# Turning the linear attention's decayed keys and output by VectorE and DMA instead of TensorE, with another split of the transfers and longer pauses

## The chip, the cores and the metric

The kernel runs on one core of one Trainium2 chip. The metric is device time in microseconds (us) of one execution. A core has TensorE (PE; its weight loads are listed apart as PEld), VectorE (DVE), ScalarE (ACT), GpSimd (POOL) and SyncE (SP), and 16 DMA engines that move data between the on-chip memory and DRAM. [...]

## The reference

Two layers, each on 256 rows of width 2048. One input projection feeds three groups of heads: A, eight heads of chunked soft-max attention; B, four heads of gated linear attention; M, four heads of cross-attention into 256 memory rows. Each group is multiplied by a SiLU gate, and one output projection and a normalisation close the layer. What matters here is group B:

```python
def step(state, inp):
    qc, kc, vc, gc = inp
    b = jnp.cumsum(gc, axis=1)
    decay = jnp.exp(-jnp.abs(b[:, :, None] - b[:, None, :]))
    attn = jnp.einsum('bihd,bjhd,bijhd->bhij', qc, kc, decay)
    o_intra = jnp.einsum('bhij,bjhv->bihv', attn, vc)
    o_inter = jnp.einsum('bihd,bhdv->bihv', qc * jnp.exp(b), state)
    b_last = b[:, -1]
    k_dec = kc * jnp.exp(b_last[:, None] - b)
    new_state = jnp.exp(b_last)[..., None] * state + jnp.einsum('bjhd,bjhv->bhdv', k_dec, vc)
    return new_state, o_intra + o_inter
...
h = x @ w_in
...
o_b = o_b * lax.rsqrt(jnp.mean(jnp.square(o_b), axis=-1, keepdims=True) + RMS_EPS) * gla_norm_g.astype(jnp.float32)
...
y = jnp.concatenate([y_a * jax.nn.silu(a_z), y_b * jax.nn.silu(b_z), y_m * jax.nn.silu(m_z)], axis=-1)
out = y @ w_out
return layer_norm(DEEPNORM_ALPHA * x + out, ln_g, ln_b)
```

`k_dec` has features in partitions when it is made, and the product over `j` needs positions there, so it must be turned. The gated output `y_b` has positions in partitions, and the output projection wants features there, so it is turned too.

## The kernel before, in words

The large projections run in **pieces**. A piece loads a slab of weights by a DMA on SP's queue (`piece`, L129), splits it into a high part (`wh`, cast by ScalarE, L117) and a low part (`wl`, by VectorE, L118), and multiplies both with the activations on TensorE (`mm`, L95). The pools of `raw`, `wh` and `wl` have four buffers each. In a layer the pieces come in the order: memory values and keys, B's queries and keys, four groups of value columns (`values`, 388 columns each), between them A's queries and keys for two groups of four heads, the memory queries, B's gate, three more gate projections, and four groups of the output projection. A group has eight pieces.

The small work (attention heads and linear attention) is put between the pieces by generators. After each piece the code calls `tick` (L52), which adds 1 to a clock (0.76 for a value piece) and lets at most one due generator run to its next `yield`; the number it yields is how many ticks it pauses. While the linear attention runs two generators are active, after that three; a finished one makes room for the next. `finish` ticks without pieces until the given generators are done. Since TensorE and SP keep the program's order, the pauses set where the small products stand in TensorE's stream. VectorE, ScalarE and GpSimd are not in that list: their order is made by a scheduler when the program is built, from dependences, priorities and its own estimate of times. In the text below pieces are counted within a layer from the first piece of B's queries and keys.

`gla` (L312) is the linear attention: gates, the cumulative sum `b_`, the decayed keys `kd` (L367 to L371), a pause of 6, then four TensorE transposes of `kd` into a PSUM bank (L397), a ScalarE copy to `kdT` (L399), a pause of 2, and the state products from `kdT`. `gla_gate` (L482) multiplies the output by its gate, and `gla_turned` (L491) turns it by eight TensorE transposes (L498) into two banks, from which ScalarE makes the scaled high part (L501) and VectorE the low part (L502) of the output projection's first operand.

`a_head` (L516) is a chunk head: scores on TensorE, soft-max on VectorE and ScalarE, `turned`, a pause of 7, then the value products from `pT` and a pause of 2. `m_head` (L546) is a memory head: scores, soft-max, `turned`, a pause of 7, two casts of `pT` (ScalarE) and two subtractions (VectorE), a pause of 2, products.

`turned` (L505) turns a tile of four 128-row blocks without TensorE: VectorE transposes each 32x32 square in one instruction (L508), and transfers through a DRAM tile `home` put the squares in their place. They are issued by GpSimd: four writes of 32 partitions each (L511), then, when they have landed, one read of the whole (L512).

Of the kernel before, what the change touches and what calls it, by code (L numbers as in the profile page):

```python
# [8 lines left out]
F32 = mybir.dt.float32  # L9
# [3 lines left out]
AF = mybir.ActivationFunctionType  # L13
ALU = mybir.AluOpType
# [4 lines left out]
P = 128  # L19
D = 2048  # L20
T = 256
L = 2
CH = 64
# [13 lines left out]
def hybrid_trunk_kernel(  # L37
# [7 lines left out]
    pe, dve, act, pool, sp = nc.tensor, nc.vector, nc.scalar, nc.gpsimd, nc.sync  # L45
# [27 lines left out]
    def enter(name, bufs=1, **kw):  # L73
        return ctx.enter_context(tc.tile_pool(name=name, bufs=bufs, **kw))
# [5 lines left out]
    hd = enter("hd", 1)  # L80
# [9 lines left out]
    def nm(s):  # L90
        uid[0] += 1
        return f"{s}_{uid[0]}"

    def mm(o, l, r, start, stop):
        pe.matmul(o, l, r, start=start, stop=stop, skip_group_check=True)  # L95

    def bank():
        return psa.tile([P, 512], F32, name=nm("bk"), tag="bk")

    def scratch(shape, dtype=F32):  # L100
        return sc.tile(shape, dtype, name=nm("sc"), tag="sc")

    def small(shape, tag, bufs=1):
        return sm.tile(shape, F32, name=nm(tag), tag=tag, bufs=bufs)

    ident = cst.tile([P, P], F32, name="ident")
# [3 lines left out]
    def operand():  # L110

        x = opp.tile([P, 4, 2, T], F32R, name=nm("x"), tag="x")
        return x[:, :, 0], x[:, :, 1], x.rearrange("p j h t -> p j (h t)")
# [198 lines left out]
    def gla(gw, gb, ng, gq, gk, lr, asv, yraw):  # L312
        gqf = gq.rearrange("p b t -> p (b t)")
        gkf = gk.rearrange("p b t -> p (b t)")
        pairs = [hd.tile([P, 4, CH], F32, name=nm("pairs"), tag=f"pairs{par}") for par in range(2)]

        def products(kl, ql, pb):

# [23 lines left out]
        pt = bank()  # L342
# [24 lines left out]
        kd = scratch([P, 512])  # L367
# [5 lines left out]
        act.activation(eb, b_, AF.Exp, scale=1.0 / 16)  # L373
        elast = small([P, 8], "elast")
        dve.tensor_copy(elast, eb.rearrange("p (g c) -> p g c", c=CH)[:, :, CH - 1])
        qe = hd.tile([P, 512], F32, name=nm("qe"), tag="qe")
        dve.tensor_tensor(qe, gqf, eb, op=ALU.mult)
        yield 6

        def decayed(s):  # L380

# [9 lines left out]
            return kl, ql  # L391


        pt = bank()
        for t in range(2):
            for b in range(2):
                pe.transpose(pt[:, (t * 2 + b) * P:(t * 2 + b + 1) * P], kd[:, b * T + t * P:b * T + t * P + P], ident)  # L397
        kdT = scratch([P, 4, P])
        act.copy(kdT, pt.rearrange("p (g c) -> p g c", c=P))  # L399
        yield 2  # L400
        nxt = [decayed(LEVELS[0])]
        kv = [bank() for _ in range(2)]
        for c in range(3):
            rs = slice((c % 2) * 64, (c % 2) * 64 + 64)
            t = c // 2
            for b in range(2):
                for par in range(2):
                    h = 2 * b + par
                    mm(kv[c % 2][par * 64:par * 64 + 64, (t * 2 + b) * P:(t * 2 + b + 1) * P],
                       kdT[rs, t * 2 + b, par * 64:par * 64 + 64],  # L410
                       asv[rs, t, 16 + h * P:16 + (h + 1) * P], True, True)

        low, high = bank(), bank()
        diagonal, first = [low[:, :256], kv[1][:, 256:]], [low[:, 256:], high[:, :256]]
        products(gkf, gqf, diagonal)
        products(*nxt[0], first)
        st = hd.tile([P, 3, 2, P], F32, name=nm("st"), tag="st")
        for c in range(3):
            t = c // 2
            src = kv[c % 2].rearrange("p (g c) -> p g c", c=P)[:, t * 2:t * 2 + 2]  # L420
# [19 lines left out]
        on = [yraw[:, 2 * par:2 * par + 2].rearrange("p c (g d) -> p (c g) d", d=P) for par in range(2)]  # L440
# [8 lines left out]
        for t in range(2):  # L449
            for b in range(2):  # L450
                g = t * 2 + b
# [5 lines left out]
        for odd, even in ((1, 2), (3, None)):  # L457
            for b in range(2):
                for c in (odd, even):
                    if c is not None:  # L460
                        for par in range(2):
                            g = (c // 2) * 2 + b
# [4 lines left out]
        for par in range(2):  # L467
# [3 lines left out]
            r = on[par][at[half], 2 - 2 * half:]  # L471
# [18 lines left out]

    def gla_turned(yraw, ng, y):  # L491

        for par in range(2):
            on = yraw[:, 2 * par:2 * par + 2].rearrange("p t (b d) -> p t b d", d=P)
            pt = bank()
            for t in range(2):
                for b in range(2):
                    pe.transpose(pt[:, b * T + t * P:b * T + (t + 1) * P], on[:, t, b], ident)  # L498
            ptv = pt.rearrange("p (b t) -> p b t", b=2)
            hi, lo = (x.rearrange("p (b r) t -> p r b t", r=2)[:, par] for x in y[:2])  # L500
            act.activation(hi, ptv, AF.Copy, scale=ng[:, 0:1])  # L501
            dve.scalar_tensor_tensor(lo, ptv, ng[:, 0:1], hi.bitcast(F32), op0=ALU.mult, op1=ALU.subtract)  # L502
            yield 1

    def turned(dst, src, n):  # L505

        blocks = scratch([P, 4, n])
        dve.transpose(blocks.rearrange("p b (g j) -> p g b j", j=32), src.rearrange("p (g b j) -> p g b j", b=4, j=32))  # L508
        home = drm.tile([P, 4, n], F32, name=nm("home"), tag=f"home{n}")
        for a in range(4):  # L510
            pool.dma_start(home[:, a].rearrange("(b i) n -> i b n", b=4), blocks[a * 32:(a + 1) * 32])  # L511
        pool.dma_start(dst, home)  # L512

    SCALE = P ** -0.5

    def a_head(h, load_bias, bias, q, k, asv, y):  # L516

        if h + 2 < 8:
            load_bias(h + 2)
        pb = bank()  # L520
        mm(pb[:, 0:128], q[:, 0:128], k[:, 0:128], True, True)
        mm(pb[:, 128:384], q[:, 128:256], k, True, True)
        s = scratch([P, 384])
        dve.scalar_tensor_tensor(s, pb[:, :384], SCALE, bias[h], op0=ALU.mult, op1=ALU.add)  # L524
        mx = small([P, 2], "mx", 4)
        zs = small([P, 2], "zs", 4)
        own = (slice(0, 128), slice(128, 384))
        for t in range(2):
            dve.tensor_reduce(mx[:, t:t + 1], s[:, own[t]], AX.X, ALU.max, negate=True)  # L529
        for t in range(2):  # L530
            act.activation(s[:, own[t]], s[:, own[t]], AF.Exp, bias=mx[:, t:t + 1], accum_out=zs[:, t:t + 1])  # L531
        dve.reciprocal(zs, zs)
        for t in range(2):
            dve.tensor_scalar(s[:, own[t]], s[:, own[t]], zs[:, t:t + 1], None, op0=ALU.mult)
        pT = tp.tile([P, 4, 96], F32, name=nm("pT"), tag="pT")
        turned(pT, s, 96)
        yield 7
        po = bank()
        v0 = 528 + h * P
        pv, pov = pT.rearrange("p a (g j) -> p g a j", j=32), po[:, :256].rearrange("p (t a j) -> p t a j", t=2, j=32)  # L540
        mm(pov, asv[:, 0, v0:v0 + P], pv[:, 0:2], True, False)
        mm(pov[:, 1], asv[:, 1, v0:v0 + P], pv[:, 2], False, True)
        act.copy(y, po[:, :256])
        yield 2

    def m_head(h, q, mk, mv, y):  # L546
# [17 lines left out]
        for t in range(2):  # L564
            dve.tensor_scalar(s[:, t], s[:, t], zs[:, t:t + 1], None, op0=ALU.mult)
        pT = hd.tile([P, 4, 128], F32, name=nm("pT"), tag="qe" if h % 2 else "gb_")
        turned(pT, s.rearrange("p t m -> p (t m)"), 128)
        yield 7
        ph, pl = scratch([P, 2, 256], F32R), scratch([P, 2, 256], F32R)
# [50 lines left out]
    def columns(n):  # L620
        return slice(n * 512, (n + 1) * 512)

    def wo_pieces(l, n):

        if n < 3:
            return [w512[l, G_WO + n, pc] for pc in range(8)]
        return [[w256[l, i, pc // 2][:, pc % 2 * 512:pc % 2 * 512 + 512] for i in range(2)] for pc in range(8)]
# [141 lines left out]
    for l in range(L):  # L769
# [20 lines left out]
        gq = hd.tile([P, 2, T], F32, name=nm("gq"), tag="gq")  # L790
        gk = hd.tile([P, 2, T], F32, name=nm("gk"), tag="gk")
# [17 lines left out]
        def heads(g):  # L809
            t = hd.tile([P, 4, T], F32, name=nm("qk"), tag="qk", bufs=4)  # L810
            for i, a, b in ws_group(w512[l, g], xq):
                total(t[:, i:i + 2], a, b)
            return t
# [14 lines left out]
        def load_bias(h):  # L828
            bias[h] = hd.tile([P, 384], F32, name=nm("bias"), tag="bias", bufs=4)
            sp.dma_start(bias[h], relw[l, h])  # L830
# [3 lines left out]
        if l > 0:  # L834
            finish(gens)
        yraw = [per.tile([P, 4, T], F32, name=nm("yr"), tag=f"yr{i}") for i in range(4)]
        gens = [[gla(*gp, gq, gk, lr, asv, yraw[0])]]
        waiting.extend(gens[0])
        linear[:] = gens[0]
        for half in range(2):  # L840
            values(2 + half)
            q = heads(G_AQ0 if half == 0 else G_AQ1)
            k = heads(G_AK0 if half == 0 else G_AK1)
# [14 lines left out]
        gla_gate(acc, yraw[0])  # L858
        yq = [operand()]
        gens[0] = [gla_turned(yraw[0], gp[2], yq[0])]  # L860
        waiting[:0] = gens[0]
        for i, g in ((1, G_AZ0), (2, G_AZ1), (3, G_MZ)):
            y = operand()
# [18 lines left out]
        for n in range(WO_N):  # L882
            if last:
                g, b = scratch([P, 512]), scratch([P, 512])
            else:
                both = per.tile([P, 2, 512], F32, name=nm("gb"), tag=f"yr{n}")
                g, b = both[:, 0], both[:, 1]
# [3 lines left out]
            src = wo_pieces(l, n)  # L891
# [30 lines left out]
            if last:  # L922
                r = res[:, 1, columns(n)]
# [90 lines left out]
```

## Time and the profile before

| | |
|---|---|
| median of 3 runs | 922.42 us (922.07 to 927.72) |
| the profiled execution's own time | 922.5 us |
| its span in the profile | 920.7 us |
| TensorE busy | 909.6 us, 99% |
| VectorE, ScalarE, GpSimd busy | 65%, 53%, 10% |
| mean granted TensorE clock | 0.995 |
| DMA | 189 MB, 206 GB/s |

The span is what the profiler saw from the first to the last instruction; the execution's own time has 1.8 us more around it. Lines of the profile name the kernel's line, the engine, the operation and the tiles as written by the program (`sc` is any scratch tile, `bk` a PSUM bank, `acc` a projection's accumulator, `yr` the heads' outputs). In the views by line the numbers after the bar are busy us, the mean ns of one, and the idle time of the engine just before, with what ended it. In the waits they are us in total, the number of waits, and the longest. In the chain a row has its start, its length and what it was. In the stretches of time each engine has its busy us and its number of instructions, then come the granted clock, the DMA share and GB/s.

### The profile page before, as it was taken

Reading aid. Unit: us, or ns where it says so; the run is one execution under the profiler, and the core shown is the slowest. Engines: PE = TensorE matmul, PEld = TensorE weight load, DVE = VectorE, ACT = ScalarE, POOL = GpSimd, SP = SyncE. Lnnn points to the kernel's source line nnn. Section 1 sums busy time; section 2 is a strip of 40 time slices with the busy share of each in tenths; the row PEclk is TensorE's granted clock in tenths of the full one; section 3 lists DMA queues with packets and bytes.
Section 4 is the critical chain, followed back from the end, with each engine's and each line's share of the span. In section 5 each row is a group of like instructions: output and inputs, shape, how many; then the busy total and the mean of one; then the engine's idle time right before and its main releaser. Section 6 shows DMA issues by size and latency. Waiting matters only on the chain.

```text
span 920.7 us, 14332 instructions
## 1 busy us (share of the span) xinstructions
PE 909.6 (99%) x5420; PEld 798.8 (87%) x5420; DVE 602.2 (65%) x845; ACT 488.7 (53%) x702; POOL 87.8 (10%) x169
## 2 busy tenths in 40 slices
PE   9999999999999999999999999999989999999997
PEld 7889998998888888888888899889878888888885
DVE  6764478656566576555587665985746676776566
ACT  6644475475455565434476445654734565654350
POOL 1000000012033030000000000001211230310000
PEclk9999999999999999999999999999999999999998
DMA  9965865558576586655774466555565775776652
GB/s 306 335 191 173 297 219 165 157 178 278 170 216 203 200 252 205 216 195 184 233 255 164 152 205 202 186 163 179 209 212 175 220 214 177 228 251 208 199 162 91
DMA packets 75989, 189.33 MB, mean 206 GB/s; under 512 B 9224, under 2 KB 33160, under 8 KB 75664
## 3 DMA queue, kind: packets, MB, share of 16 engines
q1 hardware_dynamic: 69120, 173.30, 57.7%
q0 software_dynamic: 6656, 14.86, 5.5%
q8 instruction: 42, 0.69, 0.3%
q10 hardware_dynamic: 144, 0.26, 0.1%
q14 instruction: 27, 0.22, 0.1%
HBM read 181.01 MB, written 7.34 MB: 205 GB/s over the span
## 4 chain that ended last, share of the span: by engine, by line
PE 90%; DMA 4%; ACT 2%; DVE 1%; issue 1%; POOL 1%; SPq 0%; POOLq 0%
PE acc L95 82%; PE bk L95 7%; DMA home<-sc 2%; DMA raw<-w 2%; DMA pT<-home 1%; ACT wh L117 1%; POOL home L511 1%; ACT sc L474 1%; PE bk L599 0%; DVE wl L118 0%; ACT L290 0%; PE bk L498 0%; ACT asv L807 0%; DVE mx L529 0%; DVE qk L263 0%
## 5 line engine op out<-in xcount | busy, mean ns | idle before, releaser
L118 DVE TENSOR_TENSOR wl<-raw,wh 128x1024 fp32r<-128x1024 f32 (+3 forms) x321 | 369.9, 1154 | 251.6 <-ACT wh L117 250.3
L117 ACT CAST wh<-raw 128x1024 fp32r<-128x1024 f32 (+3 forms) x321 | 318.9, 995 | 338.1 <-PE acc L95 231.8
L95 PE MATMUL acc<-x,wh 128*128 128x512 f32 x1248 | 397.1, 400 | 0.2 <-ACT wh L117 0.2
L95 PE MATMUL acc<-wh,x 128*128 128x512 f32 (+2 forms) x1236 | 356.5, 369 | 0.0
L95 PEld LDWEIGHTS acc<-x,wl 128*128 128x128 f32 x1248 | 234.7, 188 | 55.3
L95 PEld LDWEIGHTS acc<-wh,x 128*128 128x128 f32 x1236 | 227.0, 188 | 27.8 <-ACT wh L117 0.4
L95 PE MATMUL acc<-x,wl 128*128 128x256 f32 x1248 | 246.0, 278 | 0.0
L95 PE MATMUL acc<-wl,x 128*128 128x512 f32 (+2 forms) x618 | 228.0, 369 | 0.0
L95 PEld LDWEIGHTS acc<-x,wh 128*128 128x128 f32 x1248 | 192.6, 189 | 2.5 <-ACT wh L117 0.8
L95 PEld LDWEIGHTS acc<-wl,x 128*128 128x128 f32 x618 | 116.0, 188 | 15.0 <-DVE wl L118 0.8
L511 POOL DMA_DIRECT2D home<-sc x96 | 52.5, 554 | 336.6 <-DVE sc L508 333.5
L531 ACT ACTIVATE sc<-sc,mx 128x128 f32<-128x128 f32 (+1 forms) x32 | 14.3, 448 | 10.6 <-DVE mx L529 10.5
L512 POOL DMA_DIRECT2D pT<-home x24 | 13.4, 560 | 54.2 <-DMA home<-sc 49.8
L95 PE MATMUL bk<-pT,asv 128*128 128x256 f32 (+1 forms) x64 | 14.0, 342 | 4.2 <-DMA pT<-home 4.2
L95 PEld LDWEIGHTS bk<-pT,asv 128*128 128x128 f32 x64 | 11.7, 197 | 5.9 <-DMA pT<-home 4.6
L386 ACT ACTIVATE sc<-sc 128x512 f32<-128x512 f32 x12 | 7.6, 633 | 15.4 <-DVE sc L384 15.3
L508 DVE STREAM_TRANSPOSE sc<-sc 128x384 f32<-128x384 f32 (+1 forms) x24 | 14.9, 621 | 0.6
L118 DVE TENSOR_TENSOR x<-sc,x 128x512 fp32r<-128x512 f32 x20 | 13.3, 684 | 0.7 <-ACT x L117 0.7
L304 POOL DMA_DIRECT2D gwraw<-gate_w x6 | 3.1, 522 | 106.0 <-PE bk L587 105.1
L95 PE MATMUL bk<-qk,qk 128*128 128x128 f32 (+1 forms) x64 | 13.1, 326 | 0.0
L118 DVE TENSOR_TENSOR x<-res,x 128x512 fp32r<-128x512 f32 (+2 forms) x14 | 10.4, 764 | 4.0 <-ACT x L117 4.0
L524 DVE SCALAR_TENSOR_TENSOR sc<-bk,bias 128x384 f32<-128x384 f32 x16 | 8.7, 543 | 6.6 <-PE bk L95 6.5
(207 smaller groups left out, 566.3 us busy)
## 6 DMA issues: line engine op xcount, KB each, us to landing
raw<-w SPq DMA_DIRECT2D x214, 512.0 KB, 4.3
raw<-w SPq DMA_DIRECT2D x64, 388.0 KB, 3.5
raw<-w SPq DMA_DIRECT2D x83, 256.0 KB, 3.5
bias<-relw SPq DMA_DIRECT2D x16, 192.0 KB, 4.2
home<-sc POOLq DMA_DIRECT2D x64, 48.0 KB, 3.7
pT<-home POOLq DMA_DIRECT2D x16, 192.0 KB, 4.1
res<-xT SPq DMA_DIRECT2D x4, 512.0 KB, 5.0
res<-xn SPq DMA_DIRECT2D x1, 2048.0 KB, 8.2
```

What stands on the lines that cost most here:

```text
L95: pe.matmul(o, l, r, start=start, stop=stop, skip_group_check=True)
L117: act.copy(hi, src)
L118: dve.tensor_tensor(lo, src, hi.bitcast(F32), op=ALU.subtract)
L304: pool.dma_start(raw[i * 16:i * 16 + 16], gate_w[l])
L386: act.activation(dd, dd, AF.Abs)
L474: act.activation(sq, on[par][:, g], AF.Square, scale=1.0 / math.sqrt(P), accum_out=ms[:, par * 4 + g:par * 4 + g + 1])
L508: dve.transpose(blocks.rearrange("p b (g j) -> p g b j", j=32), src.rearrange("p (g b j) -> p g b j", b=4, j=32))
L511: pool.dma_start(home[:, a].rearrange("(b i) n -> i b n", b=4), blocks[a * 32:(a + 1) * 32])
L512: pool.dma_start(dst, home)
L524: dve.scalar_tensor_tensor(s, pb[:, :384], SCALE, bias[h], op0=ALU.mult, op1=ALU.add)
L531: act.activation(s[:, own[t]], s[:, own[t]], AF.Exp, bias=mx[:, t:t + 1], accum_out=zs[:, t:t + 1])
```

## The change

The decayed keys are turned by `turned` instead of TensorE, right after they are made; the pause behind them is 9 instead of 6; ScalarE's copy to `kdT` reads the landed tile with the 32-wide squares reordered, and the state products take `kdT` with the indices of half and pair exchanged. `pairs` is allocated later. The gated output is turned by two calls of `turned`, each with a pause of 6, and the scaled high and low parts are made in four steps of 128x128 each for either half, from the landed tiles. `turned` itself now makes one write of the whole tile and four reads of 32 partitions each. A chunk head pauses 9 ticks instead of 7.

```diff
@@ gla
-        pairs = [hd.tile([P, 4, CH], F32, name=nm("pairs"), tag=f"pairs{par}") for par in range(2)]
+        pairs = []
...
+        kdm = hd.tile([P, 4, P], F32, name=nm("kdT"), tag="st")
+        turned(kdm, kd, P)
         qe = hd.tile([P, 512], F32, name=nm("qe"), tag="qe")
         dve.tensor_tensor(qe, gqf, eb, op=ALU.mult)
-        yield 6
+        yield 9
...
-        pt = bank()
-        for t in range(2):
-            for b in range(2):
-                pe.transpose(pt[:, (t * 2 + b) * P:(t * 2 + b + 1) * P], kd[:, b * T + t * P:b * T + t * P + P], ident)
         kdT = scratch([P, 4, P])
-        act.copy(kdT, pt.rearrange("p (g c) -> p g c", c=P))
+        act.copy(kdT.rearrange("p g (a j) -> p g a j", j=32), kdm.rearrange("p a (g j) -> p g a j", j=32))
...
-                       kdT[rs, t * 2 + b, par * 64:par * 64 + 64],
+                       kdT[rs, b * 2 + t, par * 64:par * 64 + 64],
...
+        pairs.extend(hd.tile([P, 4, CH], F32, name=nm("pairs"), tag=f"pairs{par}") for par in range(2))
@@ gla_turned
+        yT = []
         for par in range(2):
-            on = yraw[:, 2 * par:2 * par + 2].rearrange("p t (b d) -> p t b d", d=P)
-            pt = bank()
+            yT.append(hd.tile([P, 4, P], F32, name=nm("yT"), tag=("gq", "gk")[par]))
+            turned(yT[par], yraw[:, 2 * par:2 * par + 2].rearrange("p t d -> p (t d)"), P)
+            yield 6
+        for par in range(2):
             for t in range(2):
                 for b in range(2):
-                    pe.transpose(pt[:, b * T + t * P:b * T + (t + 1) * P], on[:, t, b], ident)
-            ptv = pt.rearrange("p (b t) -> p b t", b=2)
-            hi, lo = (x.rearrange("p (b r) t -> p r b t", r=2)[:, par] for x in y[:2])
-            act.activation(hi, ptv, AF.Copy, scale=ng[:, 0:1])
-            dve.scalar_tensor_tensor(lo, ptv, ng[:, 0:1], hi.bitcast(F32), op0=ALU.mult, op1=ALU.subtract)
+                    hi, lo = (x.rearrange("p k (t a j) -> p k t a j", t=2, j=32)[:, b * 2 + par, t] for x in y[:2])
+                    src = yT[par].rearrange("p a (t b j) -> p t b a j", t=2, j=32)[:, t, b]
+                    act.activation(hi, src, AF.Copy, scale=ng[:, 0:1])
+                    dve.scalar_tensor_tensor(lo, src, ng[:, 0:1], hi.bitcast(F32), op0=ALU.mult, op1=ALU.subtract)
             yield 1
@@ turned
-        for a in range(4):
-            pool.dma_start(home[:, a].rearrange("(b i) n -> i b n", b=4), blocks[a * 32:(a + 1) * 32])
-        pool.dma_start(dst, home)
+        pool.dma_start(home, blocks)
+        for b in range(4):
+            pool.dma_start(dst[b * 32:(b + 1) * 32], home[:, b].rearrange("(a i) n -> i a n", a=4))
@@ a_head
         turned(pT, s, 96)
-        yield 7
+        yield 9
```

## The prediction

> **What bounds the kernel now.** I read the page's busy times and clock first, then the waits, then the chain that ended last in order of time.
>
> ```profile
> span 920.7 us, 14332 instructions
> PE 909.6 (99%) x5420; PEld 798.8 (87%) x5420; DVE 602.2 (65%) x845; ACT 488.7 (53%) x702; POOL 87.8 (10%) x169
> ...
> PEclk9999999999999999999999999999999999999998
> ```
>
> TensorE is never short of work except for 11 us of the span. The waits say where:
>
> ```profile
> PEld bk L95 <- DMA pT<-home: 4.6, 2, 3.0
> ...
> PE acc L95 <- ACT wh L117: 0.2, 1, 0.2
> ACT wh L117 <- PE acc L95: 231.8, 163, 2.8
> ```
>
> There are two real waits in the middle of the program, one per layer, and both are for pT, a chunk head's turned probabilities (4.6 us by the weight loads, which are the first to be held). Everything else feeds TensorE in time: ScalarE's weight cast waits 163 times for TensorE to free a buffer, so ScalarE is as far ahead as four buffers let it be. So time can be won in two ways only: fewer TensorE instructions, or those two waits. The chain gives both their place:
>
> ```profile
> 132.49 0.44 PE bk L397 x4
> ...
> 175.87 2.12 PE acc L95 x12
> ...
> 226.60 3.44 DMA pT<-home
> 230.08 0.92 PE bk L95 x4
> 231.00 16.73 PE acc L95 x96
> ...
> 251.83 2.78 PE acc L95 x16
> 254.62 0.66 PE bk L95 x4
> ...
> 316.84 0.44 PE bk L498 x4
> ...
> 323.32 0.71 PE bk L95 x6
> ...
> 679.01 4.75 DMA pT<-home
> 683.81 1.65 PE bk L95 x4
> 685.46 17.33 PE acc L95 x96
> ```
>
> Four transposes take 0.44 us of TensorE; a piece of 16 products takes 2.78, one of 12 narrow ones 2.12; a chunk head's score or value products 0.66, a memory head's 0.71. The wait at 230.08 and that at 683.81 stand before the same thing, the value products of chunk head 3: counted by the tick rule they come after six pieces (x96) and before the scores of head 4. The second wait costs more than itself. The same four products then take 1.65 instead of 0.92 us and the next 96 take 17.33 instead of 16.73: 1.3 us. The clock shows why:
>
> ```profile
> 683.80:687.20 3.40, 3.39 (x12) 2.93 (x13) 0.00 (x0) 0.37 (x1) 0.00 (x0) 0.58 0.52 169
> 230.10:233.50 3.40, 3.40 (x19) 2.99 (x20) 0.69 (x1) 0.37 (x1) 0.00 (x0) 1.00 0.63 223
> ```
>
> After the 3.0 us wait the granted clock was 0.58 over 3.4 us and 12 matmuls went through; after the shorter wait of layer 0 it stayed 1.00. [...]
>
> **The change, part by part.** *Transposes removed.* Each layer loses four at L397 and eight at L498, 24 in all, six groups of 0.44 us: **-2.6 us**. All lie between products of the pieces, on the path. No matmul is added: the products that read kdT are the same with another index.
>
> *What takes their place.* Per layer three turnings more (kd, and the output twice): three VectorE transposes of 128x512, 15 GpSimd DMAs, and ScalarE and VectorE work on other operands.
>
> ```profile
> L508 DVE STREAM_TRANSPOSE sc<-sc 128x512 f32<-128x512 f32 x8 | 5.7, 710 | 0.2
> L501 ACT ACTIVATE x<-bk,ng 128x512 fp32r<-128x512 f32 x4 | 2.7, 684 | 0.0
> L502 DVE SCALAR_TENSOR_TENSOR x<-bk,ng,x 128x512 fp32r<-128x512 f32 x4 | 3.0, 744 | 0.0
> L474 ACT ACTIVATE sc<-yr x16: 303/311/313, 192.8 to 649.7; 128x128 f32<-128x128 f32 x16
> ```
>
> VectorE gains 3 x 0.71 us per layer. The kdT copy stays one instruction. The two 128x512 steps on each engine in the output become eight of 128x128; no row has that form, and between a quarter of 684 ns (no cost per instruction) and the 311 ns of a 128x128 square on ScalarE (L474) lie the bounds; I take 0.35, a little over the upper one for the stepped source: 2.8 instead of 1.4 us on each engine per layer. Cover: ScalarE is busy 53%, VectorE 65%, and both only have to stay ahead of TensorE by the weight buffers. **0**, as long as neither is held.
>
> kd's chain: the turning starts some 0.7 us after kd, and its first consumer now comes nine pieces later instead of six, plus two as before. Write, wait, reads and landing add up to 0.55 + 4 + 2.2 + 4, about 11 us, from the rows below, and nine pieces of 2.12 us are 19 us at the least. GpSimd has nothing else then:
>
> ```profile
> 181.90 2.20 POOL L511 DMA_DIRECT2D home<-sc  x4 [63.52 <-DVE sc L508]
> ```
>
> It sits idle for 63.5 us before the first head's turning at 181.9. **0**.
>
> The pauses move everything behind them on TensorE: I counted the ticks again. gla ends four pieces later (at the 61st piece of the layer's tick count instead of the 57th), chunk heads 1, 2, 3 then issue their scores in pieces 61, 62, 63 (before 57, 59, 60) and their value products in 70, 71, 72 (before 64, 66, 67). Heads 4 to 7 and the memory heads follow two pieces later than before, and the last step of the output falls in the last piece but one of the gates (111 of 112). Nothing spills into an emptied `finish`, so TensorE has a piece to work on at each step.
>
> *A turning with one write and four reads.* Same five issues, same bytes.
>
> ```profile
> home<-sc POOLq DMA_DIRECT2D x64, 48.0 KB, 3.7
> pT<-home POOLq DMA_DIRECT2D x16, 192.0 KB, 4.1
> ```
>
> An issue takes GpSimd about 0.55 us (the timeline rows further down, four in 2.2); the large transfer lands in 4.1 us and the small in 3.7; which is the write changes the sum by nothing I can see: 0.55 + 4.1 + 2.2 + 3.7 against 2.2 + 3.7 + 0.55 + 4.1. TensorE must now wait on four landings per head instead of one; a semaphore instruction there takes 51 ns:
>
> ```profile
> L599 PEldq EVENT_SEMAPHORE  x4: 51/51/51, 476.4 to 489.6; - x4
> ```
>
> Three more for 16 chunk heads is 2.4 us at most if each is felt, 0 if they run while the array is busy, as this row's four do: they appear nowhere among TensorE's waits. I take 0.
>
> *The wait of chunk head 3.* This is the largest term, so here is the chain on GpSimd (timeline of POOL, layer 0):
>
> ```profile
> 203.43 2.21 POOL L511 DMA_DIRECT2D home<-sc  x4 [12.61 <-DVE sc L508]
> 208.59 0.56 POOL L512 DMA_DIRECT2D pT<-home  x1 [2.94 <-DMA home<-sc]
> 212.66 2.18 POOL L511 DMA_DIRECT2D home<-sc  x4 [3.50 <-DVE sc L508]
> 218.92 0.56 POOL L512 DMA_DIRECT2D pT<-home  x1 [4.08 <-DMA home<-sc]
> 219.47 2.18 POOL L511 DMA_DIRECT2D home<-sc  x4
> 226.60 0.56 POOL L512 DMA_DIRECT2D pT<-home  x1 [4.95 <-DMA home<-sc]
> ```
>
> the score products of heads 1, 2 and 3 on TensorE:
>
> ```profile
> 196.72 0.82 PE L95 MATMUL bk<-qk,qk 128*128 128x128 f32 x4
> ...
> 203.60 0.82 PE L95 MATMUL bk<-qk,qk 128*128 128x128 f32 x4
> ...
> 207.04 0.82 PE L95 MATMUL bk<-qk,qk 128*128 128x128 f32 x4
> ```
>
> GpSimd turns the heads one after the other and sleeps in between for each write. Call t the scores of head 1. Now: first write t+6.7, third read issued t+29.9, landed 3.44 later, t+33.3; TensorE was ready 1.6 us before. After: the value products of head 3 come 11 pieces behind t with five small groups between, 11 x 2.78 + 5 x 0.66 = t+33.9. GpSimd: t+6.7, then three times 0.55 + the write's wait + 2.2. With the mean of the three waits (2.94, 4.08, 4.95: 4.0) the last read has been issued by t+27.0 and lands 2.9 us later (3.44 - 0.56): t+29.9, 4 us early. With 4.95 each time and the slower landing of layer 1 (4.75 - 0.56) it is t+34.0, even. So both waits and the slow clock go: **-4.6 - 1.3 = -5.9 us**, bounds -5.9 (a wait cannot go below nothing) and 0.
>
> **The sum**: 922.5 (the profiled execution's own time, 1.8 over its span, 0.1 over the median of the runs shown) - 2.6 - 5.9 = **914.0 us**, 0.9% less. What is late next: nothing on TensorE that the trace shows.
>
> **Rivals.** *Head 3 still waits.* The scores of heads 1, 2, 3 now come 3.4 us apart, so VectorE and ScalarE have three soft-max chains at once; if that makes the first write 2 us later, t+31.8 to t+36 stands against t+33.9. At the mean nothing, at the worst 2 us per layer and no slow clock: 914 + 1 to 914 + 4, say **917**. For it: head 2 took 9.1 us from its scores (203.60) to its first write (212.66), head 1 6.7. Against: GpSimd, not VectorE, was last for head 3.
>
> *The queue hands the wait on.* The output's two turnings are ready right behind the last chunk head and memory heads 0 and 1. If they get ahead of a memory head on GpSimd's queue, each puts some 7 us before it (0.55 + 4 + 2.2), and the head has about 4 us over. A wait of 3 us in each layer, each with 1.3 of slow clock, gives back 8.6: **922.6**, no change. For it: nothing in the code ties GpSimd's order to the order of the text. Against: in the text the heads come first.
>
> *Slower: ScalarE is held at the last output turning.* Its place: ScalarE's eight scaled copies of the output read the landed tile, and the weight casts queue behind them. The four buffers give TensorE three pieces of lead, 8.3 us. A memory head's tile is turned 8.4 us after its scores (323.32 above, and the row below). If both output turnings go behind memory heads 2 and 3, whose scores come one and two pieces after the step that turns the output, four turnings of 7 us begin 11.5 us after that step and the last lands at 43.5, where the output projection wants it at 14 x 2.78 + 4 x 0.71 = 41.8. ScalarE, if the copy stands in its queue 16 us early, holds the casts 8 us beyond the lead; with 1.3 for the clock TensorE loses 9 to 10 us in each layer: 914 + 20 = **934**. It decides from 8.8 us a layer. For it: GpSimd's serial chain as above. Against: the memory heads' copies, which wait the same way, held ScalarE 4.0 us in 4 waits, 1.1 at most:
>
> ```profile
> 331.01 0.71 DVE L508 STREAM_TRANSPOSE sc<-sc 128x512 f32<-128x512 f32 x1
> ...
> ACT sc L117 <- DMA pT<-home: 4.0, 4, 1.1
> ```
>
> [...]
>
> *It doesn't do what it says* only as far as the waits go: the transposes leave TensorE in every case; alone they give 919.9, which lies inside the first two rivals.
>
> **How the numbers follow.** Forecast 914.0: 0.62, with its own range 912 to 916 (run-to-run 0.2%). Head 3 still waits, 917: 0.11. Handed on, 922.6: 0.10. ScalarE held, 934: 0.17. A measurement of this kernel tells about 1% from no change: below 913.2 is faster, over 931.6 slower. The forecast lies 0.8 above that bound, so I give half of its chance (0.31) to either side; the other 0.31 with the two middle rivals is 0.52 for within 1%, and 0.17 is slower. The range 911.5 to 925 leaves out the last rival and a little.
>
> **What would show it.** Right: no L397 and L498 groups, 5,396 TensorE matmuls; no wait of TensorE on pT, no stretch of lower granted clock in the middle; 30 more turning issues on GpSimd (150 for 120), TensorE's first output products without a wait. Wrong: a wait before value products or memory heads (first two rivals), ScalarE waiting on yT for more than 8 us, or pieces of more than 2.8 us beside the four landings' semaphores.

## The result, and the profile after

| | median us | runs | ratio to before, 95% interval |
|---|---|---|---|
| before | 923.15 (922.07 to 927.72) | 6 | |
| changed | 918.11 (917.29 to 919.21) | 6 | 0.9938 (0.9916 to 0.9960) |

The changed kernel is 0.6% faster; the forecast was 0.9% (914.0). The 918.1 lies in the range, 911.5 to 925, and within 1% of the time before. The profiled execution took 918.0 us, its span 916.2.

First the page of the changed kernel, the same rows as before:

```profile
span 916.2 us, 14372 instructions
PE 907.1 (99%) x5396; PEld 795.2 (87%) x5396; DVE 608.0 (66%) x863; ACT 489.9 (53%) x714; POOL 104.2 (11%) x199
...
PEclk9999999999999999999999999999999999999999
```

TensorE has 24 instructions fewer, 5,396, and GpSimd 30 more (199 for 169), both as foretold. Then what it waited for (us in total, times, longest):

```profile
PEld acc L95 <- DVE wl L118: 4.4, 7, 1.0
...
PEld acc L95 <- ACT wh L117: 2.2, 6, 0.5
...
PE acc L95 <- DVE wl L118: 1.6, 3, 0.5
```

No row for pT is left: both waits of before are gone, and with them the stretch of half clock (3.4 us in layer 1 at a granted clock of 0.50; now it is 1.00 up to 911 us). In their place stands something that before had hardly any of: TensorE waits for weights, for the low parts from VectorE and the high parts from ScalarE. The timeline of TensorE, layer 0, has it right behind the scores of chunk head 3 (215.24):

```profile
215.24 0.82 PE L95 MATMUL bk<-qk,qk 128*128 128x128 f32 x4
215.93 0.73 PE L95 MATMUL acc<-x,wh 128*128 128x512 f32 x2
217.19 0.50 PE L95 MATMUL acc<-x,wl 128*128 128x256 f32 x2 [0.52 <-DVE wl L118]
...
220.07 0.73 PE L95 MATMUL acc<-x,wh 128*128 128x512 f32 x2 [0.28 <-ACT wh L117]
221.33 0.51 PE L95 MATMUL acc<-x,wl 128*128 128x256 f32 x2 [0.53 <-DVE wl L118]
```

The idle times in brackets understate it, since ends of matmuls are modelled: a wl pair that otherwise starts 0.46 us behind its wh pair comes 1.26 us behind it here, twice (215.93 to 217.19, 220.07 to 221.33). ScalarE's timeline says what its casts waited for:

```profile
202.25 1.04 ACT L117 CAST wh<-raw 128x1024 fp32r<-128x1024 f32 x1
...
214.83 1.04 ACT L117 CAST wh<-raw 128x1024 fp32r<-128x1024 f32 x1 [2.74 <-DMA raw<-w]
...
218.97 1.05 ACT L117 CAST wh<-raw 128x1024 fp32r<-128x1024 f32 x1 [2.21 <-DMA raw<-w]
```

Between 203.3 and 214.8 us there is no weight cast, and two of the next ones, 214.83 and 218.97, wait for the transfer of their weights. So one step further back, to SP's queue, on which those transfers are issued (the changed kernel's timeline of SP):

```profile
191.89 0.33 SPq L142 DMA_DIRECT2D raw<-w  x1
210.78 0.33 SPq L831 DMA_DIRECT2D bias<-relw  x1
211.20 10.44 SPq L142 DMA_DIRECT2D raw<-w  x6
```

and that of the kernel before:

```profile
185.27 0.34 SPq L142 DMA_DIRECT2D raw<-w  x1
198.55 0.33 SPq L830 DMA_DIRECT2D bias<-relw  x1
198.97 6.94 SPq L142 DMA_DIRECT2D raw<-w  x5
```

SP issues nothing for 18.9 us: it stands at the load of a bias (L831 in the changed kernel, L830 before), and the weights queue behind. Among SP's waits the row is, before and after:

```profile
SPq L830 <- DVE sc L524: 25.9, 2, 12.9
```

```profile
SPq L831 <- DVE mx L530: 37.7, 2, 18.9
```

A chunk head `h` begins with `load_bias(h + 2)`, into one of four buffers. The load for head 5 stands in head 3's text, and its buffer is head 1's: it must wait until VectorE has added that bias to head 1's scores (done at 210.75). Before, heads 1 and 3 stood three pieces apart and SP was held 12.9 us; now they stand two apart and behind gla's last step, and it is 18.9.

### The profile page after: what moved, and what is told of

Its sections match the earlier page's. It is cut to its first block, busy times and chain, and to the rows that moved or that the text cites. A ratio compares the mean times of both kernels' runs of the same rounds, so it can differ in the third digit from the quotient of the medians.

```text
span 916.2 us, 14372 instructions
## 1 busy us (share of the span) xinstructions
PE 907.1 (99%) x5396; PEld 795.2 (87%) x5396; DVE 608.0 (66%) x863; ACT 489.9 (53%) x714; POOL 104.2 (11%) x199
## 4 chain that ended last, share of the span: by engine, by line
PE 93%; ACT 2%; DMA 2%; DVE 1%; SPq 0%; issue 0%; ACTq 0%
PE acc L95 86%; PE bk L95 7%; DMA raw<-w 2%; ACT sc L473 1%; ACT wh L117 1%; PE bk L600 0%; ACT yr L468 0%; DVE yr L479 0%; ACT L290 0%; DVE wl L118 0%; DVE yr L471 0%; ACT qk L262 0%; DVE sc L525 0%; SPq L165 0%; SPq L178 0%
## 5 line engine op out<-in xcount | busy, mean ns | idle before, releaser
L513 POOL DMA_DIRECT2D pT<-home x96 | 52.4, 552 | 51.9 <-DMA home<-sc 16.6
L511 POOL DMA_DIRECT2D home<-sc x30 | 16.8, 559 | 345.5 <-DVE sc L509 336.7
L532 ACT ACTIVATE sc<-sc,mx 128x128 f32<-128x128 f32 (+1 forms) x32 | 14.3, 449 | 13.7 <-DVE mx L530 13.7
L391 DVE TENSOR_TENSOR sc<-gk,sc 128x512 f32<-128x512 f32 x12 | 8.2, 686 | 8.1 <-ACT sc L389 8.1
```

Of the source, the lines that this page charges most:

```text
L391: dve.tensor_tensor(kl, gkf, dd, op=ALU.mult)
L511: pool.dma_start(home, blocks)
L513: pool.dma_start(dst[b * 32:(b + 1) * 32], home[:, b].rearrange("(a i) n -> i a n", a=4))
```

## The experiments

Two theories on the 4 us between the forecast and 918.1. **Queue**: SP is held at the bias and the weights come late. **ScalarE**: its casts are late because gla's last step (copies, squares, two table loads of 1.28 us) and three soft-maxes lie close together. "Changed" and "before" name the two kernels above.

**1. Changed, the bias loaded four heads ahead.**

```diff
-        if h + 2 < 8:
-            load_bias(h + 2)
...
         yield 9
+        if h + 4 < 8:
+            load_bias(h + 4)
...
-        load_bias(0)
-        load_bias(1)
+        for h in range(4):
+            load_bias(h)
```

> The changed kernel, with the bias of a chunk head loaded four heads ahead, behind the head's pause, into a buffer that has long been read (four loads at the start), so that no load on SP's queue waits for another head's scores. Queue theory: the two TensorE waits on wl and wh behind head 3's scores came from SP's queue, where head 5's bias waited for head 1's scores (18.9 us) with the weight loads behind it; they go, 4 us in all, 913.5 to 914.5 us, and no waits of TensorE on wl or wh between 205 and 225 us. ScalarE theory: the casts were late because ScalarE was busy with gla's last step (eight squares, two table loads) and three soft-maxes; the waits stay at 1 to 2.5 us per layer, 916 to 918 us.

Measured: 914.31 us (913.82 to 914.97), ratio 0.9909 (0.9886 to 0.9932). The last waits of TensorE in the middle of the program come to one of 0.4 us:

```profile
PE bk L95 <- DVE eps L769: 1.1, 1, 1.1
PE acc L95 <- ACT wh L117: 0.4, 1, 0.4
PE bk L95 <- ACT nparts L117: 0.3, 1, 0.3
```

gla's last step, the three soft-maxes and their places in TensorE's stream are the same as in the changed kernel. Head 3's value products come 27.1 us behind its scores in either layer, against 29.4 (215.24 to 244.60) and 28.4 us (667.21 to 695.61) in the changed kernel: 2.3 and 1.3 us, so 3.6 of the 3.8 us between the two medians lie in this stretch.

One reservation: ScalarE's order is made anew with each build, and here three weight casts stand behind the one of 202 us and ahead of head 1's soft-max, where the changed kernel has none:

```profile
205.15 1.03 ACT L117 CAST wh<-raw 128x1024 fp32r<-128x1024 f32 x1
...
208.88 1.03 ACT L117 CAST wh<-raw 128x1024 fp32r<-128x1024 f32 x1
...
211.68 1.05 ACT L117 CAST wh<-raw 128x1024 fp32r<-128x1024 f32 x1 [1.76 <-PE acc L95]
```

So the experiment alone does not part the held queue from that order. The changed kernel's rows above do: ScalarE was idle for 2.74 and 2.21 us before its late casts, until weights that SP had issued from 211.20 on had landed. The queue theory holds, and 914.3 is near the forecast's 914.0. With experiment 7 this is the fastest kernel here.

**2. Changed, pause behind the decayed keys 6 instead of 9.**

```diff
         dve.tensor_tensor(qe, gqf, eb, op=ALU.mult)
-        yield 9
+        yield 6
```

> The changed kernel with the pause behind the decayed keys put back from 9 to 6. By the tick count gla then ends at pieces 54 and 57 as before, heads 1, 2, 3 issue their scores at 57, 58, 62 instead of 61, 62, 63. Queue theory: head 3, which asks for the bias that waits for head 1's scores, comes five pieces behind head 1, so the weight loads are not held; no waits of TensorE on wl or wh there, and none on pT (value products at 66, 67, 71); 913.5 to 915.5 us. ScalarE theory: gla's last step and the scores of heads 1 and 2 lie just as close, so the waits stay at 2 to 4 us in all; 916 to 918 us. Beside both: kdT is read six pieces after its turning, which may hold ScalarE or TensorE for some us; then a wait on kdT shows at 130 to 145 us.

Measured: 929.36 us (926.84 to 931.17), ratio 1.0072 (1.0047 to 1.0097). The times of both theories left out what the last sentence of the expectation allows for, a wait on kdT, and that wait decided:

```profile
PE bk L95 <- ACT sc L397: 11.0, 2, 7.1
...
PE acc L95 <- ACT wh L117: 1.0, 3, 0.6
```

On the question it was made for it agrees with the queue: with heads 1 and 3 five pieces apart SP is held 7.9 us per layer and weights cost TensorE 1.0 us of idle time, though the waits on kdT before them blur this. On the cover of kd's turning, the time that it has to spare, it is plain. In the changed kernel ScalarE's copy ran at

```profile
141.05 0.62 ACT L397 COPY sc<-kdT 128x512 f32<-128x512 f32 x1 [1.85 <-DMA kdT<-home]
```

and in layer 1 at

```profile
595.74 0.62 ACT L397 COPY sc<-kdT 128x512 f32<-128x512 f32 x1 [4.57 <-DMA kdT<-home]
```

with the state products at 146.62 and 598.60: 5.0 and 2.2 us over. Three pieces are 8.3 us, so without them about 3 and 6 us must be missing; it was 3.9 and 7.1. The clock fell too: behind the first wait two wh products took 1.22 us (at 146.14) where they otherwise take 0.62, and the mean granted clock of the profiled execution was 0.990, against 0.998 in the changed kernel.

**3. Before, with only the chunk heads' pause of 9.**

```diff
         turned(pT, s, 96)
-        yield 7
+        yield 9
```

> The kernel before with the chunk heads' pause of 9 instead of 7 and nothing else. By the tick count heads 1, 2, 3 issue their scores at pieces 57, 58, 62 and their value products at 66, 67, 71. Both theories: the waits on pT go with the slow clock, 5.9 us: 916 to 917.5 us. Queue theory: no wait on wl or wh, since head 3 stands five pieces behind head 1. ScalarE theory: gla's last step and two heads together leave waits on wl or wh of 2 us or more: 918 to 920 us.

Measured: 916.56 us (916.22 to 917.11), ratio 0.9933 (0.9911 to 0.9956), no wait on pT, and on weights:

```profile
PE acc L95 <- ACT wh L117: 0.9, 3, 0.4
```

The term of 5.9 us is right to half a us (922.77 - 916.56 = 6.2), and one number alone, the 9, brings as much as the whole change did. gla's last step and two heads lie together here too, and weights cost 0.9 us where the ScalarE theory asked for 2 or more: against that theory. SP's hold became shorter as well, 7.9 us a layer instead of 12.9, so this run does not say whether the pause or the shorter hold removed the wait on pT; experiments 4 and 6 bear on that.

**4. Changed, with the chunk heads' pause of 7.**

```diff
-        yield 9
+        yield 7
```

> The changed kernel with the chunk heads' pause of 7 as before. Heads 1, 2, 3 issue their scores at 60, 61, 62 and their value products at 67, 68, 69, nine pieces and some 28 us behind head 1, while GpSimd's chain ends 30 to 34 us behind it. Both theories: head 3 waits for pT 2 to 6 us per layer, which may take the place of part of the wait on weights. Queue theory: the weights' wait stays, since heads 1 and 3 stand two pieces apart; 921 to 928 us. ScalarE theory: the same.

Measured: 938.13 us (935.12 to 941.78), ratio 1.0163 (1.0131 to 1.0195). The direction is as expected, the size is not (921 to 928 expected); beyond pT and the weights a memory head waited as well:

```profile
PE bk L95 <- DMA pT<-home: 9.3, 3, 3.8
PE acc L95 <- DVE wl L118: 3.9, 4, 1.8
PE bk L95 <- ACT sc L117: 3.1, 1, 3.1
```

The waits on pT alone are what was expected for two layers; the rest is the weights, the third row, and a lower clock, 0.989 in the mean of the profiled execution against 0.998 in the changed kernel. The third row is a memory head whose tile was late, at 357 us in layer 0. It looks like the rival "handed on" of the prediction, but the output's turning did not get ahead of it: the head's write left GpSimd first (338.70, the output's 339.89), landed only after 9.5 us (the median of such writes is 4.8), and its reads left right behind that (348.79). Why that write took so long stays open. SP was held about as long as in the changed kernel (18.2 against 18.9 us), so with such a hold a pause of 7 is too short: the change is sound only together with its longer pause.

**5. Changed, with three bias buffers.**

```diff
-            bias[h] = hd.tile([P, 384], F32, name=nm("bias"), tag="bias", bufs=4)
+            bias[h] = hd.tile([P, 384], F32, name=nm("bias"), tag="bias", bufs=3)
```

> The changed kernel with three bias buffers instead of four: a head's load two ahead now waits for the scores of the head just before it, one piece back, and head 7's load at head 5 waits for head 4 in the same way. Queue theory: SP is held at head 2 already, one piece (2.8 us) earlier, and again at heads 3 and 5; TensorE's waits on wl and wh grow from 4 us in all to 10 to 25 us: 924 to 940 us, with new waits behind heads 4 to 6. ScalarE theory: no more work on ScalarE, 918 us.

Measured: 936.68 us (929.54 to 940.82), ratio 1.0144 (1.0101 to 1.0186):

```profile
PE acc L95 <- ACT wh L117: 10.6, 5, 3.0
PE acc L95 <- DVE wl L118: 2.6, 4, 1.4
```

and among SP's own waits

```profile
SPq L831 <- DVE mx L530: 89.0, 6, 21.3
```

SP's hold grew from 37.7 to 89.0 us, and TensorE's wait for weights with it, in layer 0 at 215 and, behind head 5, at 257 us. The engines have no more to do than in the changed kernel. With experiment 1 and the rows of the changed kernel this shows the queue theory from both sides.

**6. Before, with only the bias loads moved** (the edit of experiment 1, with the pause of 7).

> The kernel before with only the bias loads moved (four heads ahead, behind the pause). Queue theory: SP's hold of 12.9 us for a bias goes, but TensorE did not wait for weights there, so nothing comes of it: the two waits on pT stay, 4 to 6 us with the slow clock; 920 to 923 us. ScalarE theory: the same time.

Measured: 917.04 us (916.66 to 918.05), ratio 0.9939 (0.9916 to 0.9962). Both theories gave the wrong time: the waits on pT are gone, with a pause of 7 and the old split. GpSimd's timeline shows where the time came from:

```profile
205.08 2.21 POOL L511 DMA_DIRECT2D home<-sc  x4 [14.87 <-DVE sc L508]
210.40 2.17 POOL L511 DMA_DIRECT2D home<-sc  x4 [3.11 <-DVE sc L508]
...
223.98 0.56 POOL L512 DMA_DIRECT2D pT<-home  x1 [4.95 <-DMA home<-sc]
```

and TensorE's shows head 3's value product, which waits for nothing now:

```profile
228.38 0.81 PE L95 MATMUL bk<-pT,asv 128*128 128x256 f32 x4
```

Head 2's tile is written from 210.40 instead of 212.66 and head 3's read leaves at 223.98 instead of 226.60, 2.6 us earlier, though head 1's write came 1.65 us later. Before, the weights released at 198.97 came close together, VectorE split four of them between 204.3 and 210.5, and head 2's soft-max stood between those:

```profile
207.15 0.55 DVE L524 SCALAR_TENSOR_TENSOR sc<-bk,bias 128x384 f32<-128x384 f32 x1
...
209.28 1.22 DVE L118 TENSOR_TENSOR wl<-raw,wh 128x1024 fp32r<-128x1024 f32 x1
...
211.01 0.15 DVE L532 RECIPROCAL zs<-zs 128x2 f32<-128x2 f32 x1
```

Here the same first and last steps stand at

```profile
205.81 0.55 DVE L522 SCALAR_TENSOR_TENSOR sc<-bk,bias 128x384 f32<-128x384 f32 x1
...
208.74 0.17 DVE L530 RECIPROCAL zs<-zs 128x2 f32<-128x2 f32 x1 [0.73 <-ACT sc L529]
```

1.3 of the 2.3 us lie ahead of head 2's first step on VectorE (207.15 against 205.81); the rest comes from VectorE's order, which the scheduler made differently in the two builds: before, two more steps (the split at 209.28 and L263) stood ahead of the reciprocal. So the wait on pT went with the place of the bias loads; whether by the hold itself or by the order made around it is not separated.

**7. Experiment 1 with the old split of a turning** (four writes, one read).

```diff
-        pool.dma_start(home, blocks)
-        for b in range(4):
-            pool.dma_start(dst[b * 32:(b + 1) * 32], home[:, b].rearrange("(a i) n -> i a n", a=4))
+        for a in range(4):
+            pool.dma_start(home[:, a].rearrange("(b i) n -> i b n", b=4), blocks[a * 32:(a + 1) * 32])
+        pool.dma_start(dst, home)
```

> The kernel of the first experiment (changed kernel, bias four heads ahead) with the old split of a turning: four writes and one read. Taken as not mattering: 914 us, within 1 us of the first experiment's 914.3, no TensorE waits in the middle. If the new split is what lets the third head's tile come in time: waits on pT of 1 us or more per layer and 916 us or more.

Measured: 914.11 us (913.78 to 914.32), ratio 0.9905 (0.9880 to 0.9931), against 914.31 with the new split: off the path the split does not matter.

**8. Before, with only the new split.**

> The kernel before with only the new split of a turning: one write and four reads. Taken as neutral: the two waits on pT stay at 3 to 6 us in all, 921 to 924 us. In the profile after, one of the four reads took 4.8 us to land where the single read took 4.1 and a small write 3.7, so a turning may be 1 us longer: then the waits grow by 1 us each, with a slow clock in both layers, 924 to 927 us.

Measured: 925.02 us (920.87 to 931.27, 12 runs), ratio 1.0036 (1.0009 to 1.0063). On the path the new split costs 0.8 to 5.8 us by the interval, about 3 in the median. The profiled execution was one of the quicker (922.9) and shows only a hint, 4.4 us of idle time where before has 4.2, and the landings (KB each, median us):

```profile
home<-sc POOLq DMA_DIRECT2D x16, 192.0 KB, 3.4
pT<-home POOLq DMA_DIRECT2D x64, 48.0 KB, 4.4
```

Which part of a turning is longer in the slower executions stays open.

## Why the prediction was right, and where it was not

**Transposes: right.** -2.6 us were foretold. Experiments 6 and 1 differ by the change without the wait on either side: 917.04 - 914.31 = 2.7 us. The pause and the split differ between them too; the pairs that were measured side by side, 3 against 1 and 6 against 7, give 2.3 and 2.9.

**The wait of chunk head 3: right in size, in part by luck.** -5.9 us were foretold; the longer pause as the only edit gave 6.2 us (experiment 3), and in the changed kernel the wait's rows and the half clock are gone. But the cause was only half named. I put it down to GpSimd turning one head after the other; that chain is there, but with the bias loads moved the same chain with the same pause is in time (experiment 6).

And the 4 us that the prediction saw to spare were not there in the changed kernel. The prediction has head 3's last read landed at t+29.9 at the mean and t+34.0 at worst, and the value products at t+33.9, with t the scores of head 1. In layer 0 (t = 208.36) the reads, their time to landing (the view of that tile) and the products are

```profile
236.08 2.17 POOL L513 DMA_DIRECT2D pT<-home  x4 [6.18 <-PE acc L95]
```

```profile
DMA to landing us min/median/max: 4.1/4.8/5.1
```

```profile
244.60 0.81 PE L95 MATMUL bk<-pT,asv 128*128 128x256 f32 x4
```

The last of the four reads landed at 242.3, which is t+33.9. In layer 1 (t = 660.34) it landed at 695.4, t+35.1, and the products stand at 695.61. Head 1's write alone had taken 7.7 and 7.2 us to land, beside the weights that SP had let through together. Late weights had put TensorE back by 2.3 and 1.3 us; without that, and with the same landings, the products would have stood at 242.3 and 694.3, just in time in one layer and 1.1 us too early in the other. That no wait on pT shows is luck. So the tile was as late as the rival "Head 3 still waits" has it (t+31.8 to t+36), and its 917 is nearer to 918.1 than the forecast; but the wait of that rival did not occur, and the time went to the weights. With the bias loads moved (experiment 1) the last read landed at t+27.8 and t+31.2, and the working of the prediction holds.

**"What is late next: nothing on TensorE": wrong, and this is the missing 4 us** (918.1 - 914.3 = 3.8 by experiment 1, 3.6 of it in the stretch named there). The failing step is the paragraph on the pauses. It counted the new places of scores and value products, and that TensorE had a piece at each step, but not what else a moved head issues: `load_bias(h + 2)` on SP, in whose queue the weights stand. Head 3's load waits for head 1's scores, and the count in the prediction had the two of them at 61 and 63 instead of 57 and 60. The row that gave the warning was in the trace before, the 12.9 us on L830, the largest single hold of SP in that stretch; it made TensorE wait for no weights then, so no TensorE row pointed to it.

**The covers: right, with less over than thought.** ScalarE's and VectorE's steps of the output took

```profile
L502 ACT ACTIVATE x<-yT,ng 128x128 fp32r<-128x128 f32 x16 | 4.9, 388 | 0.0
L503 DVE SCALAR_TENSOR_TENSOR x<-yT,ng,x 128x128 fp32r<-128x128 f32 x16 | 4.4, 343 | 0.0
```

388 and 343 ns against 350 foretold. kd's chain (start of VectorE's transpose 128.66 to the end of the copy 141.67) took 13 us with the copy against 11 foretold without it; in layer 1 it took 14.3 and had 2.2 us to spare.

**The rival on ScalarE did not come to pass.** The profile names the output's tile in one wait of ScalarE:

```profile
357.52 0.71 ACT L117 CAST sc<-pT 128x256 fp32r<-128x256 f32 x2 [3.99 <-DMA yT<-home]
...
364.82 2.44 ACT L502 ACTIVATE x<-yT,ng 128x128 fp32r<-128x128 f32 x8
```

But the cast behind that wait reads a memory head's tile, whose last read landed at 357.4; the first read of the output's tile landed at 357.7, after the cast had begun. So it was a memory head that held ScalarE, for 4.0 us, inside the lead of three pieces (before, 1.1 at most). The scaled copies of the output waited for nothing: their tile had landed at 360.1. They ended at 367.26, and the output projection began at 367.71. The detour took over ten us of latency (13 and 14.3 for kd's chain), and the pauses paid for it.

**The split: neutral off the path, as taken, but not equal.** A small read lands in 4.8 us in the changed kernel, where I had put 3.7 from the small write; experiment 8 shows that this is felt where the turning is waited for.

## What to carry to other kernels

When work is moved in a program, list every queue on which it issues something, and for each the buffer that the issue waits for: here one small load that waited in order held the large ones behind it for 18.9 us, and the engine that starved was two steps away. Before lengthening a pause to cover a late tile, look whether the tile is still late when such a hold is taken away; here moving eight small loads gave as much as the whole change, and both together 0.9%. A hold that shows in no wait of the bounding engine today (12.9 us on SP) is the first thing to check against a change of order.

## What the runs showed of the hardware

Some waits came with a lower clock, beside their own length. In the kernel before, TensorE waited 2.8 us for pT in layer 1; from about 683.3 us, half a us before that wait ended at 683.81, its granted clock was 0.50 for 3.4 us, and from 686.9 on it was 1.00 again. Behind the wait of 1.4 us in layer 0, which ended at 230.08, it stayed 1.00. In the changed kernel, whose waits in the middle are 0.5 us at most, it was 1.00 up to 911 us. The mean granted clock of the profiled execution, the end of the program included, was 0.990, 0.989 and 0.990 in experiments 2, 4 and 5, whose longest waits are 7.1, 3.8 and 3.0 us, and 0.997 to 0.999 in experiments 1, 3, 6 and 7, where none in the middle is over 0.7. Which waits cost clock, and whether their length decides it, was not shown: no run was made for it.

I had not expected the four small reads to land later than one read of the same bytes (4.8 us in the changed kernel and 4.4 in experiment 8, against 4.1 before).
